# A ring of seven gather buffers instead of four, and four routing steps ahead of the first gather

## The chip, the cores and the metric

One Trainium2 chip, one of its cores. TensorE (PE) multiplies matrices, with its weight loads shown apart as PEld; VectorE (DVE), ScalarE (ACT) and GpSimd (POOL) do the elementwise work; SyncE (SP) issues most of the transfers, POOL those whose rows are picked by an index. The metric is the device time of one execution in microseconds (us), as the median of several runs.

## The reference, cut to what matters

One layer of an encoder over 512 tokens of 1024 numbers: an attention and gating half, and then PEER, a lookup of single-neuron experts. The change touches only PEER:

```
def peer(h, w_q, keys, U, V):              # h: 512 x 1024; U, V: 16384 x 1024
    ...                                    # scores against 2 x 128 keys, for 8 heads
    v1, i1 = lax.top_k(s1, 16)
    v2, i2 = lax.top_k(s2, 16)
    sc, ci = lax.top_k(cand, 16)           # cand: the 16 x 16 sums of v1 and v2
    idx = i1[ci // 16] * 128 + i2[ci % 16] # 8 heads x 16 experts a token
    gates = jax.nn.softmax(sc, axis=-1)
    u_sel = U[ids]
    a = jnp.einsum('chkd,cd->chk', u_sel, xb)
    w = jax.nn.gelu(a, approximate=False) * g
    return jnp.einsum('chk,chkd->cd', w, V[ids])
```

The layer ends with a root-mean-square norm of the sum of PEER's output (times a gate) and the residual.

## The kernel before, in words

PEER is done in two ways at once. For 352 tokens it is dense: TensorE multiplies all 16384 rows of U with the tokens (tiles a, block by block of 128 experts), a mask of gates g is multiplied in, and the products w go through all rows of V into six accumulators in PSUM (out). For the other 160 tokens the rows that the routing picked are gathered: the last 128 tokens (set "g", 128 rows each) and 32 tokens whose 128 picks are spread over four partitions each (set "x", 32 gathers). A gather brings one row of 1024 numbers to each of 128 partitions, 512 KB in all, by an indirect transfer that POOL issues; VectorE then makes a dot product of it with the token (gather_u, tile scr), or adds it, scaled, to a sum (gather_v, tile acc). There are 32 + 32 gathers for x and 128 + 128 for g.

The main loop runs over e, the 128 blocks of experts. In each e TensorE does 18 matmuls into out (v times w, in three products of high and low parts: vh, vl, wh, wl) and, for the first 98, 24 matmuls of dense_a(e + 30) (uh, ul). ScalarE makes the high parts, VectorE the low ones (u..l and w..l at L82, v..l at L1063) and the product a with g (L1066). Raw u has three buffers, raw v two, and so have the high and the low parts of u and v.

Everything for the gathered tokens stands in one list, fill, with a cost for each entry. A due time grows with each e, and entries are taken from the list, in its order, when it is their turn; they are issued after that e's v..l (issue_after). The list holds, first, the 32 gather_u of x, with one step of the routing of the g tokens behind each of the first 30 of them (16 of gb_keys, a table step, 8 of route_pick, one decode, two lookups, the gates, and gb_idx, which closes the routing's memory and opens the pool gpool2 in its place); then the gather_v of x, gather_u and gather_v of g, and the output of those tokens. VectorE runs all this in the order in which it is issued, along with its u..l, v..l and w..l: where it waits for a gathered row, they wait behind it. SyncE's queue carries u, v and g; POOL's queue in this stage carries nothing but gathers, each of which waits until VectorE has read its buffer.

Of the kernel before, what the change touches and what calls it, by code (L numbers as in the profile page):

```python
# [9 lines left out]
F32 = mybir.dt.float32  # L10
# [9 lines left out]
P = 128  # L20
D = 1024
# [12 lines left out]
XS = NS // XQ  # L34
# [27 lines left out]
def tile_kernel(ctx: ExitStack, tc: tile.TileContext, a: dict, out: bass.AP):  # L62
# [3 lines left out]
    def pool(st, name, side=None, space=None):  # L66
        kw = {} if space is None else {"space": space}
        return st.enter_context(tc.tile_pool(name=name, bufs=1, side=side, reuse_waits="tile", **kw))
# [706 lines left out]
    with ExitStack() as gs:  # L775
# [63 lines left out]
        for k in range(nu):  # L839
            e = ahead + k  # L840
            s0 = k * NG // nu
            st = {}
# [30 lines left out]
    st = {}  # L873
# [19 lines left out]
    def gb_idx():  # L893
# [2 lines left out]
        st["stack"].close()  # L896
        st["gp2"] = pool(ctx, "gpool2")

    def gather(src, ix, s, name):
        g = gp.tile([P, D], F32, name=name, tag="g", bufs=4)  # L900
        nc.gpsimd.indirect_dma_start(out=g, out_offset=None, in_=src,  # L901
                                     in_offset=bass.IndirectOffsetOnAxis(ap=ix[:, s:s + 1], axis=0))
        return g
# [14 lines left out]
    def gather_u(k, ix, gt_, n, ns):  # L918
        if n == 0:
            g_open(k, ns)  # L920
        g = gather(a["peer_u"], ix, n, f"gu{k}{n}")
        actg, wg = gs_[k]["act"], gs_[k]["w"]
        scr = gp.tile([P, D], BF16, name=f"scr{k}{n}", tag="scr", bufs=1)
        nc.vector.scalar_tensor_tensor(scr, g, 1.0, gs_[k]["h2g"], op0=ALU.mult, op1=ALU.mult,  # L924
                                       accum_out=actg[:, n:n + 1])
        if n == ns - 1:
            nc.scalar.activation(wg, actg, AF.Gelu)
            nc.vector.tensor_mul(wg, wg, gt_)

    def gather_v(k, ix, s):  # L930
        g = gather(a["peer_v"], ix, s, f"gv{k}{s}")
        if s == 0:
            gs_[k]["acc"] = (gp if k == "x" else st["gp2"]).tile([P, D], F32, name=f"acc{k}")
        accg, wg = gs_[k]["acc"], gs_[k]["w"]
        if s == 0:
            nc.vector.tensor_scalar_mul(accg, g, wg[:, 0:1])
        else:
            nc.vector.scalar_tensor_tensor(accg, g, wg[:, s:s + 1], accg, op0=ALU.mult, op1=ALU.add)  # L938
# [21 lines left out]
    def o_load(b):  # L960
        n = rows[b][1] - rows[b][0]
        if b in (1, 2):
            xr = vp.tile([P, D], F32, name=f"xr{b}", tag="vr", bufs=2)
        else:
            xr = gp.tile([P, D], F32, name=f"xr{b}", tag="g", bufs=4)
        nc.sync.dma_start(xr[:n], x2d[rows[b][0]:rows[b][1], :])
        if b in ("x", GB):
            y = gp.tile([P, D], F32, name=f"yf{b}", tag="g", bufs=4)
        else:
            y = up.tile([P, D], F32, name=f"yf{b}", tag="ur", bufs=3)  # L970
        ss = gp.tile([P, 2], F32, name=f"ssf{b}", tag="ssf", bufs=2)
        yg = st["gp2"].tile([P, 512], F32, name=f"yg{b}", tag="yg", bufs=2)
        outp[b] = (xr[:n], y[:n], ss[:n], yg[:n], n)

    def o_sum(b, hf):
# [23 lines left out]
    def output(b):  # L999
        o_load(b)  # L1000
        o_sum(b, 0)
        o_gain(b)
        o_sum(b, 1)
        o_root(b)
        o_store(b)

    route = []
# [8 lines left out]
        route.append((5.0, lambda f=f: route_lookup(st["r"], f, st["i"][f])))  # L1016
    route.append((1.2, lambda: route_gates(st["R"], st["sc"], gtg, PH)))
    route.append((0.3, gb_idx))
    fill = []
    for n in range(XS):  # L1020
        fill.append((1.3, lambda n=n: gather_u("x", idxx, gtx, n, XS)))
        if n < len(route):
            fill.append(route[n])
    fill += route[XS:]
    for n in range(XS):
        fill.append((1.3, lambda n=n: gather_v("x", idxx, n)))
    for n in range(NS):
# [13 lines left out]
    gp = pool(ctx, "gpool")  # L1041
# [44 lines left out]
    for b in range(ND):  # L1086
        o_load(b)
# [71 lines left out]
```

## Time and profile before

| | |
|---|---|
| time, median of 3 runs | 1548.93 us (1538.43, 1548.93, 1552.24) |
| the profiled execution's own time | 1542.68 us |
| its span, first to last instruction | 1540.8 us |
| PE busy | 1452.5 us, 94% of the span |
| DVE busy | 1279.7 us, 83% |
| POOL busy | 455.7 us, 30% |
| read from HBM, written | 381.24 MB, 28.28 MB: 266 GB/s over the span |

The profile is of one execution. A busy PE is not a PE at its peak, so the pace of the main loop is better read from the count of its matmuls in a stretch: one e of the first 98 is 42 of them, a later one 18. The main loop runs from 598.24 us to the end; what stands before it is the attention half, the routing of the dense tokens and the building of their gates.

### The profile page before, as it was taken

The page shows a single profiled execution, that of the slowest core. Times are in us where ns is not written, and L with a number is a line of the kernel's source. Part 1 is how long each engine was busy: PE and PEld are TensorE (multiplying, and loading weights), DVE is VectorE, ACT ScalarE, POOL GpSimd, SP SyncE. Part 2 cuts the span into 40 slices and gives each one's busy share as a digit, 9 for nine tenths or more (in the row PEclk, how much of TensorE's full clock was granted, in tenths as well). Part 3 has the DMA queues.
Part 4 walks back from the last instruction along what each step waited for, and adds up shares of the span by engine and source line. Part 5 has one row for each costly group of instructions (what it writes and reads, how often), then busy time and mean ns, then how long its engine had stood idle before and what let it go on. Part 6 is the DMA issues. An engine that isn't in the chain of part 4 may idle for free.

```text
span 1540.8 us, 21600 instructions
## 1 busy us (share of the span) xinstructions
PE 1452.5 (94%) x7623; PEld 1240.4 (81%) x7623; DVE 1279.7 (83%) x2476; ACT 638.9 (41%) x1078; POOL 455.7 (30%) x400
## 2 busy tenths in 40 slices
PE   2899999999979999999999999999999999999997
PEld 1765687887869999888888888888888888877775
DVE  6937865569899997899888888988888889888776
ACT  2543433434258895333433333333333333333333
POOL 1212100000000002222344554555545445444420
PEclk9899999999989999999999999999999999999999
DMA  9626343331235789899699999999999999998973
GB/s 368 228 93 221 122 150 137 131 98 57 97 117 148 217 241 302 309 334 326 226 358 369 367 348 360 367 361 363 357 364 361 360 361 359 374 323 298 313 266 118
DMA packets 154332, 410.94 MB, mean 267 GB/s; under 512 B 13008, under 2 KB 58720, under 8 KB 154096
## 3 DMA queue, kind: packets, MB, share of 16 engines
q1 hardware_dynamic: 100720, 216.49, 40.3%
q0 software_dynamic: 51568, 187.17, 33.7%
q10 hardware_dynamic: 1936, 5.90, 1.0%
q8 instruction: 60, 0.98, 0.3%
q14 instruction: 48, 0.39, 0.1%
HBM read 381.24 MB, written 28.28 MB: 266 GB/s over the span
## 4 chain that ended last, share of the span: by engine, by line
PE 41%; DMA 24%; DVE 16%; issue 10%; ACT 4%; POOL 4%; SPq 0%; POOLq 0%; DVEq 0%; ACTq 0%
DMA gug<-peer_u,idx 10%; DMA gvg<-peer_v,idx 8%; PE out L86 4%; PE out L87 4%; PE out L88 4%; PE pa L88 3%; PE pa L87 3%; PE pa L86 3%; POOL gvg L901 2%; DMA wada<-w_ada 2%; PE gg L822 2%; ACT o L816 2%; POOL gug L901 2%; PE q L87 1%; PE q L88 1%
## 5 line engine op out<-in xcount | busy, mean ns | idle before, releaser
L901 POOL DMA_INDIRECT gug<-peer_u,idx x128 | 169.8, 1327 | 147.5 <-DVE scrg L924 123.2
L901 POOL DMA_INDIRECT gvg<-peer_v,idx x128 | 160.2, 1251 | 170.1 <-DVE accg L938 145.7
L924 DVE SCALAR_TENSOR_TENSOR scrg<-gug,h2gg 128x1024 bf16<-128x1024 f32 x128 | 156.4, 1222 | 45.7 <-DMA gug<-peer_u,idx 44.6
L938 DVE SCALAR_TENSOR_TENSOR accg<-gvg,wgg,accg 128x1024 f32<-128x1024 f32 x127 | 163.0, 1284 | 28.8 <-DMA gvg<-peer_v,idx 27.6
L901 POOL DMA_INDIRECT gux<-peer_u,idxx x32 | 41.4, 1293 | 439.5 <-DMA u34r<-u_t 342.1
L822 PE MATMUL gg<-o,o 128*128 128x128 f32 x704 | 87.9, 279 | 2.7 <-ACT o L816 1.6
L822 PEld LDWEIGHTS gg<-o,o 128*128 128x128 f32 x704 | 85.5, 195 | 4.6 <-ACT o L816 4.6
L1066 DVE TENSOR_TENSOR a<-a,g 128x352 f32<-128x352 f32 x128 | 64.7, 516 | 3.5 <-ACT g L833 2.2
L816 ACT ACTIVATE o<-o1b,gT 128x128 f32<-128x128 bf16 x176 | 58.1, 404 | 12.9 <-PE gg L822 7.4
L155 DVE SCALAR_TENSOR_TENSOR macc<-wada,csil,macc 128x1024 f32<-128x1024 f32 x40 | 51.2, 1281 | 9.5 <-DMA wada<-w_ada 9.2
L526 ACT ACTIVATE a<-pa 128x352 f32<-128x352 f32 x128 | 58.3, 456 | 1.5 <-PE pa L88 1.4
L901 POOL DMA_INDIRECT gvx<-peer_v,idxx x32 | 41.3, 1292 | 55.8 <-DVE accx L938 32.1
L805 DVE TENSOR_TENSOR o<-iota_s,gT 128x1024 f32<-128x1024 f32 x44 | 53.5, 1216 | 0.5 <-PE gg L822 0.4
L809 DVE TENSOR_SCALAR o<-iota_s,gT 128x128 f32<-128x128 f32 x176 | 48.8, 338 | 0.0
L938 DVE SCALAR_TENSOR_TENSOR accx<-gvx,wgx,accx 128x1024 f32<-128x1024 f32 x31 | 39.8, 1284 | 8.7 <-DMA gvx<-peer_v,idxx 8.5
L831 ACT COPY st<-gg 128x512 f32<-128x512 f32 x88 | 46.2, 580 | 0.0
L924 DVE SCALAR_TENSOR_TENSOR scrx<-gux,h2gx 128x1024 bf16<-128x1024 f32 x32 | 38.7, 1210 | 4.9 <-DMA gux<-peer_u,idxx 4.9
L141 POOL DMA_DIRECT2D wada<-w_ada x32 | 17.1, 535 | 60.6 <-DVE macc L155 25.2
L165 PE MATMUL mcol<-ident_s,macc 128*128 128x128 f32 x32 | 7.2, 383 | 27.4 <-DVE macc L152 23.2
L165 PEld LDWEIGHTS mcol<-ident_s,macc 128*128 128x128 f32 x32 | 5.2, 194 | 29.1 <-DVE macc L152 18.1
L430 ACT ACTIVATE pe<-s,mx 128x512 f32<-128x512 f32 x16 | 11.0, 689 | 29.6 <-DVE mx L428 21.6
L120 POOL TENSOR_TENSOR n_r<-n_ms,nhalf 128x1 f32<-128x1 f32 (+1 forms) x5 | 3.6, 715 | 54.3 <-DVE n_ms L118 54.3
(2817 smaller groups left out, 4980.5 us busy)
## 6 DMA issues: line engine op xcount, KB each, us to landing
gd<-st SPq DMA_DIRECT2D x11, 1984.0 KB, 9.1
g<-gd SPq DMA_DIRECT2D x31, 704.0 KB, 7.6
wada<-w_ada POOLq DMA_DIRECT2D x32, 512.0 KB, 4.7
wada<-w_ada SPq DMA_DIRECT2D x16, 512.0 KB, 10.1
x<-x SPq DMA_DIRECT2D x4, 512.0 KB, 12.1
x<-x ACTq DMA_DIRECT2D x4, 512.0 KB, 5.0
x2d<-x ACTq DMA_DIRECT2D x4, 512.0 KB, 2.7
gug<-peer_u,idx POOLq DMA_INDIRECT x128, 7.4
```

Source lines behind the costliest of these rows:

```text
L86: nc.tensor.matmul(o, lhsT=lh, rhs=rh, start=first, stop=False)
L87: nc.tensor.matmul(o, lhsT=lh, rhs=rl, start=False, stop=False)
L88: nc.tensor.matmul(o, lhsT=ll, rhs=rh, start=False, stop=last)
L155: nc.vector.scalar_tensor_tensor(acc, w, csil[:, c:c + 1], acc, op0=ALU.mult, op1=ALU.add)
L526: nc.scalar.activation(t, p[:, :TD], AF.Gelu)
L805: nc.vector.tensor_tensor(o2s[n], iota.unsqueeze(1).to_broadcast([P, UT, P]), tT[:, 1, t0:t0 + UT].unsqueeze(2).to_broadcast([P, UT, P]), ...
L816: nc.scalar.activation(o1s[n][:, i, :], e[:, :, i], AF.Copy, scale=tT[:, 2, t0 + i:t0 + i + 1])
L822: nc.tensor.matmul(pgs[n][i // 4][:, i % 4 * P:(i % 4 + 1) * P], lhsT=o2[:, i, :], rhs=o1[:, i, :], start=True, stop=True)
L901: nc.gpsimd.indirect_dma_start(out=g, out_offset=None, in_=src, in_offset=bass.IndirectOffsetOnAxis(ap=ix[:, s:s + 1], axis=0))
L924: nc.vector.scalar_tensor_tensor(scr, g, 1.0, gs_[k]["h2g"], op0=ALU.mult, op1=ALU.mult, accum_out=actg[:, n:n + 1])
L938: nc.vector.scalar_tensor_tensor(accg, g, wg[:, s:s + 1], accg, op0=ALU.mult, op1=ALU.add)
L1066: nc.vector.tensor_tensor(wv3, wv3, gt[:, :, e % GE, :], op=ALU.mult)
```

## The change

Three things. The gathers take their buffers by a counter: of each seven, three (counter modulo 7 is 1, 3 or 5) go to three buffers of a new tag, g2, in gpool2, and four to the old ones, as soon as gpool2 exists; until then all go to the old four. The output's half tile yg, which had two buffers of its own in gpool2, shares the tag g2. And four routing steps stand at the head of the list, so that the routing ends four gathers earlier in it.

```diff
+    ring = [0]
+
     def gather(src, ix, s, name):
-        g = gp.tile([P, D], F32, name=name, tag="g", bufs=4)
+        ring[0] += 1
+        if "gp2" in st and ring[0] % 7 in (1, 3, 5):
+            g = st["gp2"].tile([P, D], F32, name=name, tag="g2", bufs=3)
+        else:
+            g = gp.tile([P, D], F32, name=name, tag="g", bufs=4)
...
-        yg = st["gp2"].tile([P, 512], F32, name=f"yg{b}", tag="yg", bufs=2)
+        yg = st["gp2"].tile([P, 512], F32, name=f"yg{b}", tag="g2", bufs=3)
...
-    fill = []
+    lead = 4
+    fill = route[:lead]
     for n in range(XS):
         fill.append((1.3, lambda n=n: gather_u("x", idxx, gtx, n, XS)))
-        if n < len(route):
-            fill.append(route[n])
-    fill += route[XS:]
+        if n + lead < len(route):
+            fill.append(route[n + lead])
+    fill += route[XS + lead:]
```

Three places show what this does to the order. The first is VectorE at the fourth e. MAX, MAX_INDEX and MATCH_REPLACE are routing steps, scrx4 uses the fifth gathered row gux4, and u34l is the low part that TensorE needs for dense_a(34). Before, scrx0 to scrx3 stand just ahead of these rows:

```order
L924 SCALAR_TENSOR_TENSOR scrx4_5639,actx_5467<-gux4_5637,h2gx_5462 128x1024
L542 MAX v12g_5395<-tmpg011_5631 128x8
L539 MAX v12g_5395<-sgb2_5619 128x8
L543 MAX_INDEX i12g_5396<-v12g_5395,tmpg011_5631 128x8
L540 MAX_INDEX i12g_5396<-v12g_5395,sgb2_5619 128x8
L541 MATCH_REPLACE tmpg020_5705<-v12g_5395,sgb2_5619 128x128
L924 SCALAR_TENSOR_TENSOR scrx5_5713,actx_5467<-gux5_5711,h2gx_5462 128x1024
L542 MAX v12g_5395<-tmpg020_5705 128x8
L82 TENSOR_TENSOR u34l_5718<-u34r_5715,u34h_5717 128x1024
```

And in the changed kernel, from the first gathered row to the same u34l:

```order
L931 SCALAR_TENSOR_TENSOR scrx0_5561,actx_5557<-gux0_5559,h2gx_5552 128x1024
L542 MAX v12g_5395<-tmpg021_5637 128x8
L931 SCALAR_TENSOR_TENSOR scrx1_5635,actx_5557<-gux1_5633,h2gx_5552 128x1024
L543 MAX_INDEX i12g_5396<-v12g_5395,tmpg021_5637 128x8
L82 TENSOR_TENSOR w3l_5684<-a3_2443,w3h_5683 128x352
L931 SCALAR_TENSOR_TENSOR scrx2_5707,actx_5557<-gux2_5705,h2gx_5552 128x1024
L539 MAX v12g_5395<-sgb3_5625 128x8
L931 SCALAR_TENSOR_TENSOR scrx3_5719,actx_5557<-gux3_5717,h2gx_5552 128x1024
L540 MAX_INDEX i12g_5396<-v12g_5395,sgb3_5625 128x8
L541 MATCH_REPLACE tmpg030_5711<-v12g_5395,sgb3_5625 128x128
L82 TENSOR_TENSOR u34l_5724<-u34r_5721,u34h_5723 128x1024
```

Ahead of u34l there were six gathered rows to use, now there are four, and scrx4 and scrx5 stand behind it.

The second is POOL's queue in the long run of the g gathers; DMASW0 to DMASW7 are the eight semaphores that gathers signal in turn, and each gather waits for the one of the gather that had its buffer before it. Before:

```order
L901 DMA gug88_9823<-peer_u,idx_1854 128x1024 [waits DMASW4_49,DVE_49]
L901 DMA gug89_9889<-peer_u,idx_1854 128x1024 [waits DMASW5_49,DVE_49]
L901 DMA gug90_9893<-peer_u,idx_1854 128x1024 [waits DMASW6_49,DVE_49]
L901 DMA gug91_9897<-peer_u,idx_1854 128x1024 [waits DMASW7_49,DVE_49]
L901 DMA gug92_9963<-peer_u,idx_1854 128x1024 [waits DMASW0_49,DVE_49]
```

And now:

```order
L908 DMA gug88_9823<-peer_u,idx_1854 128x1024 [waits DMASW1_49,DVE_49]
L908 DMA gug89_9889<-peer_u,idx_1854 128x1024 [waits DMASW2_49,DVE_49]
L908 DMA gug90_9893<-peer_u,idx_1854 128x1024 [waits DMASW3_49,DVE_49]
L908 DMA gug91_9897<-peer_u,idx_1854 128x1024 [waits DMASW4_49,DVE_49]
L908 DMA gug92_9963<-peer_u,idx_1854 128x1024 [waits DMASW5_49,DVE_49]
```

The semaphore that each gather waits for moved by three: gug92 waited for the gather four ahead of it and now waits for the one seven ahead.

The third is POOL's queue where gpool2 opens, at the end of the gather_u of x. Before:

```order
L901 DMA gux26_6819<-peer_u,idxx_1856 128x1024 [waits DMASW6_49,DVE_49]
L901 DMA gux27_6892<-peer_u,idxx_1856 128x1024 [waits DMASW7_49,DVE_49]
L901 DMA gux28_7029<-peer_u,idxx_1856 128x1024 [waits DMASW0_49,DVE_49]
L901 DMA gux29_7039<-peer_u,idxx_1856 128x1024 [waits DMASW1_49,DVE_49]
L901 DMA gux30_7110<-peer_u,idxx_1856 128x1024 [waits DMASW2_49,DVE_49]
L901 DMA gux31_7114<-peer_u,idxx_1856 128x1024 [waits DMASW3_49,DVE_49]
L901 DMA gvx0_7120<-peer_v,idxx_1856 128x1024 [waits DMASW4_49,DVE_49]
```

And now:

```order
L908 DMA gux26_7032<-peer_u,idxx_1856 128x1024 [waits DMASW6_49,DVE_49]
L908 DMA gux27_7036<-peer_u,idxx_1856 128x1024 [waits DMASW7_49,DVE_49]
L908 DMA gux29_7106<-peer_u,idxx_1856 128x1024 [waits DMASW0_49,DVE_49]
L908 DMA gux31_7114<-peer_u,idxx_1856 128x1024 [waits DMASW1_49,DVE_49]
L908 DMA gux28_7040<-peer_u,idxx_1856 128x1024 [waits DMAHW3_49,DMAHW5_49,DMAHW2_49,DMAHW6_49,DMAHW1_49,Activation_49]
L908 DMA gux30_7110<-peer_u,idxx_1856 128x1024 [waits PE_49]
L908 DMA gvx0_7120<-peer_v,idxx_1856 128x1024 [waits DVE_49]
```

The first rows that go to the new buffers, gux28 and gux30, wait for what used the routing's memory, and two later gathers, gux29 and gux31, moved ahead of them.

## Rows read from the trace of the kernel before

**Rows 1.** The page: what transfers moved, in 40 slices of 38.5 us.

```profile
GB/s 368 228 93 221 122 150 137 131 98 57 97 117 148 217 241 302 309 334 326 226 358 369 367 348 360 367 361 363 357 364 361 360 361 359 374 323 298 313 266 118
```

**Rows 2.** Stretches: length, busy us (instructions) by engine, clock, DMA share, GB/s.

```profile
598.24:632.88 34.64, 31.15 (x147) 27.16 (x146) 24.17 (x78) 9.19 (x12) 12.68 (x11) 0.90 0.95 337
632.88:911.73 278.85, 278.85 (x1472) 247.12 (x1472) 254.19 (x477) 104.76 (x148) 108.52 (x83) 1.00 0.91 329
911.73:1392.46 480.73, 469.17 (x2437) 408.48 (x2437) 417.06 (x527) 169.79 (x233) 246.94 (x193) 1.00 0.96 358
1392.46:1508.57 116.11, 112.59 (x475) 84.70 (x473) 91.97 (x97) 40.58 (x54) 44.60 (x33) 0.99 0.83 286
```

**Rows 3.** Who waited for whom from 590 us on: total us, times, longest.

```profile
POOL gvg L901 <- DVE accg L938: 145.7, 88, 4.9
POOL gug L901 <- DVE scrg L924: 123.2, 84, 3.8
...
DVE scrg L924 <- DMA gug<-peer_u,idx: 44.6, 43, 3.2
...
DVE accg L938 <- DMA gvg<-peer_v,idx: 27.6, 33, 2.3
```

**Rows 4.** The same view, PE alone, from 600 to 1520 us.

```profile
PE pa L88 <- DVE u34l L82: 3.5, 1, 3.5
PE out L87 <- DVE v98l L1063: 2.6, 1, 2.6
```

**Rows 5.** TensorE in order of time: start, us, operation, [idle before it].

```profile
626.48 0.66 PE L88 MATMUL pa<-h2T,u34l 128*128 128x352 f32 x1 [3.49 <-DVE u34l L82]
626.94 0.49 PE L86 MATMUL pa<-h2T,u34h 128*128 128x352 f32 x1
627.23 0.49 PE L87 MATMUL pa<-h2T,u34h 128*128 128x352 f32 x1
```

**Rows 6.** VectorE in order of time, and POOL's fifth gather.

```profile
605.07 0.49 DVE L539 MAX8 v12g<-sgb 128x8 f32<-128x128 f32 x2 [3.98 <-DMA h2gx<-h2gd]
...
607.87 1.20 DVE L1063 TENSOR_TENSOR v2l<-v2r,v2h 128x1024 fp32r<-128x1024 f32 x1
608.99 1.21 DVE L1063 TENSOR_TENSOR v3l<-v3r,v3h 128x1024 fp32r<-128x1024 f32 x1
...
621.54 1.23 DVE L924 SCALAR_TENSOR_TENSOR scrx<-gux,h2gx 128x1024 bf16<-128x1024 f32 x1 [4.87 <-DMA gux<-peer_u,idxx]
...
625.21 1.21 DVE L82 TENSOR_TENSOR u34l<-u34r,u34h 128x1024 fp32r<-128x1024 f32 x1
...
611.62 1.87 POOL L901 DMA_INDIRECT gux<-peer_u,idxx  x1 [5.06 <-DVE v12g L539]
```

**Rows 7.** The view of tile gug: from a gather's issue to its landing.

```profile
DMA to landing us min/median/max: 4.7/7.4/10.4
```

**Rows 8.** Transfers: 880 to 1360 us in slices of 12; 3 to 36 us.

```profile
GB/s 384 348 364 325 319 372 390 326 414 370 363 374 355 352 358 367 383 315 370 369 355 324 403 334 384 366 348 403 357 337 391 328 343 392 373 341 400 332 385 348
...
3.00:36.00 33.00, 6.59 (x32) 5.13 (x32) 22.86 (x26) 5.80 (x9) 5.58 (x12) 0.99 1.02 392
```

**Rows 9.** Loads of v, us to landing: after the last gather, and among gathers.

```profile
v123r<-peer_v SPq DMA_DIRECT2D x1, 512.0 KB, 3.4
...
v112r<-peer_v SPq DMA_DIRECT2D x1, 512.0 KB, 6.3
```

**Rows 10.** VectorE's v..l, TensorE's use of it, ScalarE's cast, in order of time.

```profile
759.96 1.22 DVE L1063 TENSOR_TENSOR v21l<-v21r,v21h 128x1024 fp32r<-128x1024 f32 x1
...
768.33 0.39 PE L86 MATMUL out<-v21h,w21h 128*128 128x512 f32 x1
768.56 0.39 PE L87 MATMUL out<-v21l,w21h 128*128 128x512 f32 x1
...
1117.72 0.50 PE L87 MATMUL out<-v64l,w64h 128*128 128x512 f32 x1 [0.39 <-DVE v64l L1063]
...
1418.06 1.06 ACT L1062 CAST v103h<-v103r 128x1024 fp32r<-128x1024 f32 x1
```

## The prediction

> **What bounds the kernel now.** First I read the page's slices [rows 1]: from the middle of the span the transfers move some 360 GB/s almost without a dip, and by the stretches TensorE, VectorE and the DMA engines are all busy nine tenths of the time there [rows 2]. Any of the three could hold the main loop, and a busy share does not tell which; the count of matmuls does. In the second stretch 1472 of them, 35 steps of 42, take 278.85 us: 7.967 us a step. That is the floor, TensorE never waiting. In the third stretch, steps e = 39 to 96, 58 steps take 480.73 us, 8.288 each, so 58 x (8.288 - 7.967) = 18.6 us are lost there, in crumbs. The reader should then look at who waits [rows 3, 4]: TensorE waits for low parts that VectorE makes late, VectorE waits for gathered rows (44.6 + 27.6 us for g), and POOL, which would fetch them, waits for VectorE to free a buffer (123.2 + 145.7 us). This is a circle: buffer, transfer, use, buffer.
>
> How tight is it? In the third stretch VectorE is busy 417.06 / 58 = 7.19 us a step, so at the floor it may idle 0.78 us a step; it idles 1.10. It begins with a reserve: at e = 21 v21l is done at 761.18 us and used at 768.56, 7.4 us later, while at e = 64 TensorE waits 0.39 us for v64l [rows 10]. Between those steps the reserve was eaten, and from then on each late row costs TensorE time.
>
> The circle itself: 193 gathers in 58 steps [rows 2] are 3.33 a step, one in 8.288 / 3.33 = 2.49 us, so a buffer of four goes round in 9.96 us. Of that 7.4 us are issue to landing [rows 7] and about 1.25 the use on VectorE (a gathered dot product took 1.23 us [rows 6]), 8.65 in all. The floor needs a round of 4 x 7.967 / 3.33 = 9.57 us. On average it would fit, by 0.9 us; but landings reach 10.4 us, and a row that takes 3 us longer than the median does not.
>
> **The change, part by part.** *Seven buffers.* At the floor a buffer may now go round in 7 x 7.967 / 3.33 = 16.7 us against the same 8.65: 8.1 us of slack, more than the 3.0 us by which the latest landing exceeds the median, and more than any wait of VectorE for a row (3.2 us the longest [rows 3]). Nothing else on POOL's queue is delayed: it carries only gathers there. Whether TensorE reaches its floor then hangs on the transfers: the third stretch moved 358 GB/s x 480.73 us = 172.1 MB, which in 58 x 7.967 = 462.1 us takes 372 GB/s. The page's best slice of this stretch has 374, slices of 12 us have 400, 403 and 414, and a stretch of plain loads 392 over 33 us [rows 1, 8]. So 372 can be had, if work is always queued, which is what more buffers in flight give. Ends: nothing (the rate stays at 358) and all 18.6 us. Half way, at 366 GB/s, 172.1 MB take 470.2 us and 10.5 us are won. VectorE need not lose all its idle time, only what exceeds 0.78 us a step, so I take 16, near the upper end.
>
> *The first gathers.* At e = 3 TensorE waits 3.49 us for u34l, and then its matmuls of 352 columns start 0.29 us apart for the 22 that are left of dense_a(34) [rows 5]. Elsewhere their pace is 0.16 (a step of 7.967 less 18 matmuls at 0.23 [rows 10], over 24): the granted clock, 2.4 GHz before, was at 1.2 after the idle, which makes the stretch's mean 0.90 of full speed [rows 2]. So 3.49 + 22 x 0.13 = 6.4 us. The cause is VectorE's wait of 4.87 us for the fifth gathered row, with u34l queued behind it [rows 6]; that row could not be asked for before scrx0 had freed a buffer. In the new order u34l stands behind four rows that are already there. I walk VectorE's queue in its new order from 605.07 us with the old pace [rows 6]: eleven short instructions took the 2.80 us to v2l, 0.25 each, and v2l took 1.12. So 18 routing instructions 4.5, v2l 1.12, ten more 2.5, v3l 1.12, four rows at 1.2, w3l 0.5, five routing instructions 1.25, u34l 1.13: it ends at 622.0, and TensorE wants it when the old wait began, at 622.99. The stall goes, and the low clock with it. Next late is w4l behind scrx4: gux4 is now asked for at about 615.5, when scrx0 is done, not at 611.62, and lands after the median 7.4 us at 622.9 (after 9.9, as the old one, at 625.4); VectorE comes to scrx4 at 624.3, so w4l ends between 626.7 and 627.8, and TensorE wants it at about 626.9, 24 matmuls later. So I book 5.5 of the 6.4; ends 3 and 6.4. The reserve at the following steps is about 2 us smaller, since TensorE won more than VectorE; without more idle time it holds.
>
> *The swap on POOL.* gux28, first in a new buffer, is now issued behind gux31, which waits until scrx25 is done. From there to its landing are two issues of about 1 us and 7.4 us, against some 7 us of other work on VectorE between scrx25 and scrx28 (three long instructions and about ten short ones): a wait of 2 to 3 us. It lies at about e = 20, where the reserve is 7.4 us [rows 10]: I cost it at nothing, and at 3 us if that reserve were gone. That the routing ends four gathers earlier moves no work from one step to another but within about one of them: nothing.
>
> *The end.* In the fourth stretch 26 steps of 18 matmuls at 0.23 us [rows 10] would take 107.6 us; they take 116.11 [rows 2], 8.5 more. At its start VectorE is behind (TensorE waits 2.6 us for v98l [rows 4]); with a reserve that wait goes, the small ones later hardly. I book 4, ends 0 and 6.5. The shared g2 buffers of the output hold the same number of half tiles or more: nothing. What comes after 1508.57 us is the output and stays.
>
> **Sum** against the profiled execution's own 1542.7 us: 16 + 5.5 + 4 = 25.5 us less, 1517. The ends are 3 and 31.5 less: 1540 and 1511. That execution is 6 us under the median of the runs shown; the losses are waits that vary from run to run, which more buffers should even out, so I put the new median between 1517 and 1548.9 - 25.5 = 1523: **1520 us**, and with the forecast's own range 1508 to 1532.
>
> **The rivals.** *The transfers are full already.* Then rows arrive no faster however many are asked for: the third stretch stays at 358 GB/s, and only the first stall (5.5) and 1 or 2 us at the end are won: 1536 in the profile's time, up to 1542 as a median, say 1539. For it: a DMA share of 0.96 and a rate that hardly moves from slice to slice. Against it: the 12-us slices over 400, and the low ones between them (315, 324), which look like gaps in the asking, not a cap. The Trainium skill (HBM Reference, Specifications (TRN2)) puts a core's share of its memory at about 358 GB/s, the very rate of this stretch, and says that a core streaming alone measures well above it; by the share there would be no gain there, and the rows at 392 and more speak for the second sentence.
>
> *Slower: the gathers crowd out the v loads.* A load of v lands in 3.4 us after the last gather and in 6.3 among gathers [rows 9]. In the fourth stretch its two buffers go round in landing + 1.06 (cast) + 1.22 (low part) us [rows 10], and 2 x 4.14 = 8.3 allow a landing of 6.0: it is at the edge. If up to three more gathers in flight (1.5 MB, 4 us at 392 GB/s) were served first, a step would take (6.3 + 4 + 2.3) / 2 = 6.3 us instead of 4.3, 25 x 2 = 50 us lost there against 25 won: about 1570. It decides from a landing of about 8.3 us on, where the loss reaches 25. Against it: at the pace of VectorE's queue only 33 gathers fall in 116 us, so the mean number in flight stays, rate times landing, at 33 / 116 x 7.4 = 2.1, however many buffers there are.
>
> *The lead does not do what it says.* gux4 comes late, w4l stalls TensorE at e = 4 instead, and the clock falls again: the 5.5 becomes 0, 1526.
>
> **How the numbers follow.** Chances: forecast 0.62, full transfers 0.2, the lead without effect 0.11, slower 0.07. One per cent, 15 us, is about what a measurement of this kernel can tell from no change (its three runs span 13.8 us), so faster by over 1% means under 1533.4. Faster: 0.62 x 0.95 + 0.11 x 0.7 + a little = 0.68; slower 0.07; between, 0.25. The range reaches from the forecast's lower end, 1508, to the full-transfer case, 1541.
>
> **What would show it.** In the new profile: steps e = 39 to 96 at 8.0 to 8.05 us with 370 GB/s or more; VectorE's waits for gathers from 72 us to under 30; POOL's waits for VectorE as long or longer, but harmless, since then it has seven rows ahead; no clock under 1.00 between 600 and 640 us, and u34l ahead of TensorE's need; v loads landing in under 7 us. If VectorE's waits stay near 70 us with gathers that land in 12 us or more, the transfers were full; if e = 4 has a gap, the lead failed.

## The result, and the profile after

The changed kernel takes **1520.4 us** (median of 6 runs, 1519.5 to 1524.2) against 1547.7 us of the kernel before beside it (6 runs, 1538.4 to 1552.2): ratio 0.9856, 95% interval 0.9829 to 0.9883, 1.4% faster. The forecast was 1520 in 1508 to 1541. The profiled execution spans 1518.8 us, 22.0 less than that of before.

The first view to read is again the one by stretches, cut where TensorE begins the steps e = 0, 4, 39, 97 and 123. Columns: length, busy us (instructions) of PE, PEld, DVE, ACT and POOL, granted clock, DMA share, GB/s.

```profile
599.62:629.87 30.25, 28.53 (x146) 24.31 (x145) 21.10 (x76) 9.12 (x12) 9.70 (x8) 1.00 0.92 302
629.87:912.49 282.62, 279.77 (x1473) 246.93 (x1472) 265.51 (x490) 104.69 (x148) 128.89 (x92) 1.00 0.94 349
912.49:1374.55 462.06, 462.06 (x2437) 409.52 (x2437) 424.04 (x525) 165.84 (x233) 272.18 (x194) 1.00 0.98 373
1374.55:1486.49 111.94, 110.46 (x475) 83.86 (x473) 84.30 (x89) 40.08 (x54) 35.19 (x26) 1.00 0.74 258
```

Beside [rows 2] the four lengths change by -4.39, **+3.77**, **-18.67** and -4.17 us, in all -23.5; the loop also began 1.4 us later in this execution, which no part of the change touches. In the third stretch TensorE is busy all of its 462.06 us, 58 steps of 7.967: the floor, where TensorE never waits. One number goes the wrong way, the second stretch.

The page's slices (38.0 us each), and the shares of the chain of work that ended last, engine by engine:

```profile
PEclk9999999999998999999999999999999999999999
...
GB/s 367 233 98 206 141 153 125 132 105 67 52 164 105 227 220 267 309 327 307 268 402 400 372 376 380 379 361 378 369 387 373 380 366 378 379 357 274 306 216 117
...
PE 73%; DVE 13%; DMA 6%; ACT 4%; issue 3%; POOL 0%; SPq 0%; POOLq 0%; DVEq 0%; ACTq 0%
```

The same chain before:

```profile
PE 41%; DMA 24%; DVE 16%; issue 10%; ACT 4%; POOL 4%; SPq 0%; POOLq 0%; DVEq 0%; ACTq 0%
```

Transfers held a quarter of the chain before, and 6% of it now.

At the 21st and 22nd slice, where gathers come one behind the other, the rate is 402 and 400, above anything in [rows 1]; then it settles at 373 on average, which is what the kernel needs at its floor. In slices of 12 us, from 772 to 820:

```profile
772.00:784.00 12.00, 12.00 (x67) 10.73 (x66) 11.96 (x14) 4.30 (x6) 7.17 (x6) 1.00 1.02 409
784.00:796.00 12.00, 12.00 (x64) 10.51 (x63) 11.93 (x12) 4.27 (x6) 6.97 (x6) 1.00 1.03 409
796.00:808.00 12.00, 12.00 (x67) 10.76 (x66) 10.39 (x12) 4.29 (x6) 5.36 (x5) 1.00 1.03 409
808.00:820.00 12.00, 12.00 (x63) 10.49 (x62) 11.93 (x12) 4.28 (x6) 7.15 (x6) 1.00 1.03 411
```

Four slices at the same 409 to 411, with a DMA share of 1.02 or 1.03, look like a ceiling; an experiment below asks.

The waits of the circle [rows 3], from 590 us on, and VectorE's groups on gathered rows (count, then busy us and mean ns, then idle us before them):

```profile
POOL gvg L908 <- DVE accg L945: 141.0, 83, 6.9
POOL gug L908 <- DVE scrg L931: 72.0, 36, 4.1
...
L945 DVE SCALAR_TENSOR_TENSOR accg<-gvg,wgg,accg 128x1024 f32<-128x1024 f32 x127 | 163.8, 1290 | 1.3
...
L931 DVE SCALAR_TENSOR_TENSOR scrg<-gug,h2gg 128x1024 bf16<-128x1024 f32 x128 | 156.2, 1221 | 1.3
```

VectorE idles 1.3 + 1.3 us before the gathered rows of g, against 44.6 + 27.6 us of waits for them. By the theory below that is where the 18.7 us came from. POOL still waits 213 us for VectorE, and nobody waits for POOL.

Where the second stretch loses: PE's waits from 600 to 720 us, and VectorE in order of time around e = 3 and e = 12.

```profile
PE out L87 <- DVE v12l L1071: 1.9, 1, 1.9
PE out L88 <- DVE w3l L82: 1.7, 1, 1.7
PE out L88 <- DVE w4l L82: 0.5, 1, 0.5
PE pa L88 <- DVE u44l L82: 0.4, 1, 0.4
```

```profile
615.49 0.29 DVE L539 MAX8 v12g<-sgb 128x8 f32<-128x128 f32 x1 [3.88 <-DMA sgb<-sgd]
...
617.65 1.22 DVE L1071 TENSOR_TENSOR v3l<-v3r,v3h 128x1024 fp32r<-128x1024 f32 x1
...
621.53 0.51 DVE L82 TENSOR_TENSOR w3l<-a,w3h 128x352 fp32r<-128x352 f32 x1
...
624.96 1.23 DVE L82 TENSOR_TENSOR u34l<-u34r,u34h 128x1024 fp32r<-128x1024 f32 x1
...
691.38 0.52 DVE L82 TENSOR_TENSOR w14l<-a,w14h 128x352 fp32r<-128x352 f32 x1
695.04 0.53 DVE L1074 TENSOR_TENSOR a<-a,g 128x352 f32<-128x352 f32 x1 [3.15 <-DMA g<-gd]
695.49 1.22 DVE L1071 TENSOR_TENSOR v12l<-v12r,v12h 128x1024 fp32r<-128x1024 f32 x1
```

Two waits of VectorE are new, and neither is for a gathered row. At 611.6 it stands 3.88 us for a load of scores (sgb, the third, for the fifth routing step), with v3l, w3l and u34l behind it; at 691.9 it stands 3.15 us for a block of gates g, in front of v12l. TensorE's own waits are shorter than these, because its reserve takes the rest, but the steps e = 3 and 4 exceed their floor by 2.15 + 0.80 us (before: 6.53 and 0), and e = 12 and 13 by 2.20 + 0.76 (before: 0).

In the fourth stretch ScalarE's two longest waits for a load of v are 2.6 us for v113r and 2.5 us for v116r; here v113r, which SP issued at 1431.14:

```profile
1431.14 0.33 SPq L1063 DMA_DIRECT2D v113r<-peer_v  x1
...
1439.80 1.05 ACT L1070 CAST v113h<-v113r 128x1024 fp32r<-128x1024 f32 x1 [2.61 <-DMA v113r<-peer_v]
```

That load took 8.7 us, against 6.3 in [rows 9]. The steps e = 113 and 116 lost 1.2 and 1.0 us; before, e = 105, 111 and 116 lost 0.80, 0.45 and 0.57, with waits of the same kind.

### The profile page after: what moved, and what is told of

Read it like the earlier page. It is cut to its first block, busy times and chain, and to the rows that moved or that the text cites. A ratio compares the mean times of both kernels' runs of the same rounds, so it can differ in the third digit from the quotient of the medians.

```text
span 1518.8 us, 21628 instructions
## 1 busy us (share of the span) xinstructions
PE 1439.7 (95%) x7623; PEld 1235.6 (81%) x7623; DVE 1287.3 (85%) x2476; ACT 634.6 (42%) x1078; POOL 489.4 (32%) x400
## 4 chain that ended last, share of the span: by engine, by line
PE 73%; DVE 13%; DMA 6%; ACT 4%; issue 3%; POOL 0%; SPq 0%; POOLq 0%; DVEq 0%; ACTq 0%
PE out L86 10%; PE out L88 10%; PE out L87 10%; PE pa L88 9%; PE pa L87 9%; PE pa L86 9%; DMA wada<-w_ada 2%; PE gg L822 2%; PE q L87 1%; PE q L88 1%; PE q L86 1%; ACT o L816 1%; PE yo L87 1%; PE yo L88 1%; PE yo L86 1%
## 5 line engine op out<-in xcount | busy, mean ns | idle before, releaser
L908 POOL DMA_INDIRECT gug<-peer_u,idx x128 | 200.3, 1565 | 104.6 <-DVE scrg L931 72.0
```

## The experiments

The theory: four buffers made a round (ask, land, use, ask again) that was barely short enough, and its late rows cost the third stretch; the transfers had room. Against it stand: the new order of the work, not the ring, made the gain; the number of requests in flight, not the round, decides; the transfers are full. All ratios are to the kernel before, run on the same chip.

**The two parts alone.** *seven_no_lead*:

```
-    lead = 4
+    lead = 0
```

> Seven buffers as in the change, but no routing step ahead of the first gather. If the ring alone makes the gain of the main loop, e = 39 to 96 stays at 462 us (7.97 a step); the first stall at e = 3 comes back (6.5 us over the floor instead of 3.0 at e = 3 and 4), and if the lead caused the loss at e = 12 and 13, those 3.0 us go: about 1521, within 2 us of the changed kernel, 26 under before. If the lead was worth the 5.5 us that the prediction books, and the loss at e = 12 and 13 has another cause, it takes 1524 to 1526. If a part of the gain in the main loop came from the new order that the lead gives, the third stretch takes over 466 us and the whole over 1528.

*lead_four_buf*: the lead stays, `gather` takes all rows from the four buffers of before.

```
-        if "gp2" in st and ring[0] % 7 in (1, 3, 5):
+        if False:
```

> The lead of four routing steps with four buffers as before. If the ring makes the gain: e = 39 to 96 stays at 478 to 482 us, e = 3 and 4 together lose 3 us instead of 6.5, e = 12 and 13 lose about 3: 1545 to 1549, no difference from before. If the lead is worth what the prediction books: 1542. If the new order makes a part of the gain in the main loop: the third stretch takes under 474 us and the whole under 1541.

Seven buffers without the lead: 1519.2 us, ratio 0.9833 (0.9802 to 0.9863). The lead with four buffers: 1542.6 us, 0.9996 (0.9975 to 1.0017). Their third stretches, and behind each its fourth:

```profile
914.45:1376.51 462.06, 462.06 (x2438) 409.52 (x2437) 423.89 (x525) 165.59 (x233) 272.17 (x194) 1.00 0.99 373
1376.51:1487.58 111.07, 110.26 (x475) 83.85 (x473) 84.12 (x89) 40.05 (x54) 33.92 (x26) 1.00 0.76 260
```

```profile
912.84:1392.38 479.54, 468.36 (x2437) 408.53 (x2437) 417.51 (x529) 169.75 (x233) 242.17 (x193) 1.00 0.97 360
1392.38:1509.56 117.18, 113.10 (x475) 85.81 (x473) 92.50 (x97) 40.00 (x54) 43.54 (x33) 0.97 0.84 285
```

The whole gain of the third stretch belongs to the ring, and so does that of the fourth: 97 to 122 exceed their floor by 3.2 us with seven buffers, by 9.3 with the lead alone. The lead gives at e = 3 and 4 what it takes at e = 12 and 13: without it they lose 5.3 and 0 us, with it (four buffers) 2.6 and 2.3. The lead is worth nothing that these times can show.

**How many buffers.** The rings `% 6 in (1, 4)` with two buffers of g2, `% 5 == 1` with one, and the kernel before with three:

```
-        if "gp2" in st and ring[0] % 7 in (1, 3, 5):
+        if "gp2" in st and ring[0] % 6 in (1, 4):     # six_buf
+        if "gp2" in st and ring[0] % 5 == 1:          # five_buf
```

```
-        g = gp.tile([P, D], F32, name=name, tag="g", bufs=4)
+        g = gp.tile([P, D], F32, name=name, tag="g", bufs=3)     # three_buf
```

> The changed kernel with a ring of six buffers (four and two). By the circle (a buffer may go round in 6 x 7.967 / 3.33 = 14.4 us at the floor, against 8.65 us for landing and use and 3 us more for the latest landing) six are as good as seven: third stretch 462 to 463 us, 1519 to 1522. If what counts is how many gathers are queued at any time, a third of the gain of the main loop is lost: 468 us and about 1526.

> The changed kernel with a ring of five buffers (four and one). By the circle a buffer may go round in 5 x 7.967 / 3.33 = 12.0 us against 8.65 and 3 more for the latest landing: just enough, so nearly all of the gain stays: third stretch 462 to 466 us, 1520 to 1524. If the gain grows evenly with each buffer, two thirds of it are lost: 474 us and about 1532.

> The kernel before with three row buffers. If landing takes its 7.4 us whatever is in flight, a buffer still goes round in about 8.65 us, a row comes every 2.88 us, and the 193 rows of the third stretch take 193 x 2.88 = 556 us instead of 480; with some 30 us more in the second stretch about 1640 to 1655. If the landing time is mostly the queueing of four gathers behind each other, it falls to 5.9 us or less with three, and the kernel loses little: under 1575.

Six: 1520.0 us, 0.9843 (0.9816 to 0.9871). Five: 1520.3 us, 0.9844 (0.9814 to 0.9874). Three: 1640.7 us, 1.0649 (1.0604 to 1.0694). The third stretches, in that order:

```profile
914.70:1376.77 462.07, 462.07 (x2439) 409.55 (x2437) 423.80 (x525) 165.59 (x233) 272.65 (x194) 1.00 0.99 373
```

```profile
911.51:1373.57 462.06, 462.06 (x2437) 409.52 (x2437) 422.91 (x527) 165.59 (x233) 265.83 (x194) 1.00 0.99 373
```

```profile
937.30:1481.66 544.36, 491.85 (x2438) 423.43 (x2437) 419.80 (x530) 168.60 (x233) 229.13 (x194) 0.96 0.89 317
```

Three buffers give 544.36 / 194 = 2.81 us a row, a round of 8.4 us; the prediction had worked out 8.65 from a landing of 7.4 and a use of 1.25. The totals nearly agree, but their parts do not. With three buffers, from issue to landing (tile gug, then gvg; before, both had a median of 7.4):

```profile
DMA to landing us min/median/max: 4.2/6.3/10.2
```

```profile
DMA to landing us min/median/max: 4.3/6.0/9.7
```

The landing got shorter by more than 1 us. Followed gather by gather through the third stretch, the mean round of 8.4 us is 6.4 of landing, 0.4 until VectorE comes to the row, 1.25 of use and 0.4 until POOL issues again; before, 9.9 us were 7.4, 0.8, 1.25 and 0.5. The two waits for a turn were left out of the sum. So this time speaks for the first case of the expectation, but its condition, 7.4 us whatever is in flight, does not hold.

At the floor four buffers allow a round of 4 x 2.39 = 9.6 us and five allow 12.0. Against the 8.65 of the prediction's sum that is a slack of 0.9 and 3.3 us: with the first, four buffers lose 17 to 19 us, and with the second, five lose nothing. So the average round was short enough, and more than 0.9 us of slack was needed, which fits landings that reach 3.0 us beyond their median [rows 7]. The sixth and the seventh buffer bring nothing, where a gain that grew with each buffer would have left five at about 1532.

**How far the transfers are from full.** In the kernel with five buffers 58 more loads of rows of v, which nobody reads (the rest of the computation stays):

```
+        if 38 <= e < 96:
+            dm = st["gp2"].tile([P, 256], F32, name=f"dm{e}", tag="dm", bufs=1)    # 512, 1024
+            nc.sync.dma_start(dm, a["peer_v"][e * P:(e + 1) * P, :256])
```

> Five buffers, and at each of the steps e = 38 to 95 one more load of 128 KB (rows of v once more, read by nobody). The third stretch then has 172 + 7.6 MB to move; at TensorE's floor that is 389 GB/s. If transfers can go at the 400 of the best slices, nothing is lost: third stretch 462 to 463 us. If 373 is all they give, the stretch takes 179.7 MB / 373 GB/s = 482 us. If a fuller queue only lengthens the landing of rows, so that five buffers no longer suffice, TensorE loses up to 10 us in crumbs.

> The same with 256 KB: 187.3 MB, 405 GB/s at the floor, at the edge of what the best slices show. Transfers at 400 to 410: 462 to 468 us. Transfers at most 390: 480 us.

> The same with 512 KB: 202.5 MB, 438 GB/s at the floor, which no slice of 12 us reached. The transfers are then the bound and show their own rate: at 405 to 410 the third stretch takes 494 to 500 us. If it stays at 462, they have 438 and the limit is further off.

1587.8, 1603.0 and 1606.4 us; ratios 1.031, 1.041 and 1.043. That fits no line of what was expected: 128 KB cost some 67 us over five buffers alone, and four times as much costs 86. Most of that, 48 to 66 us, went on steps before e = 39, ahead of where the loads were meant to come. The experiment had measured something else. What SP waited for between 740 and 1000 us with 128 KB, and what ScalarE waited for:

```profile
SPq L1061 <- DMA dm<-peer_v: 194.4, 57, 6.6
```

```profile
ACT v40h L1073 <- DMA v40r<-peer_v: 13.1, 1, 13.1
ACT v29h L1073 <- DMA v29r<-peer_v: 12.9, 1, 12.9
ACT v38h L1073 <- DMA v38r<-peer_v: 12.6, 1, 12.6
```

Nothing tied the loads to their steps, so SP took all 58 loads of 128 KB between 751 and 993 us, each waiting there for the landing of the one before since they share a buffer, and the loads of u and v stood behind them. So the same with 512 KB, queued right behind the load of v of its step (*load_in_step*):

```
-        nc.sync.dma_start(vraw, a["peer_v"][e * P:(e + 1) * P, :])
+        vload = nc.sync.dma_start(vraw, a["peer_v"][e * P:(e + 1) * P, :])
+        if 38 <= e < 96:
+            dm = st["gp2"].tile([P, D], F32, name=f"dm{e}", tag="dm", bufs=1)
+            with tc.issue_after(vload.ins):
+                nc.sync.dma_start(dm, a["peer_v"][e * P:(e + 1) * P, :])
```

> Five buffers and a load of 512 KB more at each of the steps e = 38 to 95, this time queued on SP right behind the load of v of the same step, so that each comes in its own step and finds its buffer long free: 202.5 MB in the third stretch, 438 GB/s at TensorE's floor, which no slice of 12 us reached. If transfers go at 400 to 410 at most, they are the bound and show their own rate: 494 to 506 us. If 373 is all they give: 543 us. If it stays at 462 to 464, 438 can be had and the transfers were nowhere near a bound.

1551.7 us, ratio 1.0079 (1.0058 to 1.0099). The third stretch is 29.3 us longer than with five buffers alone, for 30.4 MB. The stretch, the page's slices (38.8 us each), and VectorE's and SP's waits in the stretch:

```profile
913.01:1404.33 491.32, 471.21 (x2439) 408.40 (x2437) 413.61 (x520) 166.27 (x233) 225.12 (x191) 1.00 1.02 405
```

```profile
GB/s 368 226 91 223 125 142 136 130 105 49 104 109 155 220 237 265 328 335 285 312 394 371 391 409 409 410 409 409 409 408 408 397 408 409 409 382 338 311 244 119
```

```profile
DVE scrg L931 <- DMA gug<-peer_u,idx: 43.1, 65, 2.1
DVE accg L945 <- DMA gvg<-peer_v,idx: 29.3, 36, 2.0
```

```profile
SPq L1067 <- DMA dm<-peer_v: 109.0, 47, 5.0
```

Of the twelve slices from the 24th to the 35th eleven stand at 408 to 410: here is the ceiling, 409 GB/s in this mix, the rate that the changed kernel already showed from 772 to 820 us. The changed kernel needs 373, nine tenths of it. SP waited 109 us for landings of the extra loads in this run, so it is the flat rate together with a share of 1.02, not the length alone, that makes it a ceiling. Note VectorE's waits: 43.1 and 29.3 us, against 34.8 and 27.5 in this stretch of the kernel before, from the opposite cause. There the round was too long at 358 GB/s, here the transfers are full. The sums of the waits don't tell one from the other; the rate does.

**The losses that the change brought or left.** *scores_early* puts the score loads two steps and more ahead, the third and fourth of each four into the tile that later holds the sum for x:

```
+        if h % 4 > 1:
+            st["sg"][h] = st["accx"][:, h % 4 * 256:(h % 4 + 1) * 256].rearrange("p (f n) -> p f n", n=P)
+        else:
+            st["sg"][h] = st["R"].tile([P, 2, P], F32, name=f"sgb{h}", tag="sg", bufs=2)
...
-        gb_scores(0)
+        for h in range(3):
+            gb_scores(h)
...
-        if f == 0 and h + 1 < PH:
-            gb_scores(h + 1)
+        if f == 0 and 0 < h < PH - 2:
+            gb_scores(h + 2)
```

> The changed kernel with the score loads of the lead two and more steps earlier (a third and fourth place for them in the tile that later holds the sum of x rows). If VectorE's 3.9 us wait for a score load, with v3l and u34l queued behind it, is what kept the lead from its full 5.5 us, then u34l ends about 622, e = 3 and 4 together lose under 1 us instead of 3.0, and the whole takes 3 us less than the changed kernel, about 1517. If gathered rows or the next low parts are late anyway, e = 3 and 4 still lose 2 us or more and the time stays at 1520.

*gate_late* ties the multiplication by the gates to its step:

```
+        lows.append(last)
+        with tc.issue_after(lows[max(0, e - 4)].ins):
             nc.vector.tensor_tensor(wv3, wv3, gt[:, :, e % GE, :], op=ALU.mult)
```

> The changed kernel with the multiplication of the activations by the gates (line 1074) held back on VectorE until four steps before its use; the order put it up to 28 steps ahead of use, most of that between e = 5 and 13. If that early work, and the loads of g that it waits for, ate VectorE's reserve at e = 12, the loss at e = 12 and 13 (3.0 us) goes and nothing comes back, about 1517; the last 26 steps carry 24 x 0.45 = 11 us more on VectorE, which they have idle, and lose at most 2 more. If the small reserve there comes from the lead itself, the loss stays at about 3 us or moves a few steps.

*all_three* has both, and this:

```
-        if e < NE - 3:
+        if e < NE - 3 and (e < 98 or e % 5 in (0, 2)):
             vraw = vp.tile([P, D], F32, name=f"v{e}r", tag="vr", bufs=2)
         else:
             vraw = up.tile([P, D], F32, name=f"v{e}r", tag="ur", bufs=3)
```

> Both edits, and from e = 98 on the raw rows of v take turns in five buffers (the two of v and the three of u, which are free then). If the three losses are apart from each other: 3 us at e = 3 and 4, 3 us at e = 12 and 13 and 2 us at e = 113 and 116 go, about 1512, 36 under before. If they share VectorE's reserve so that one takes the place of another: 1516 to 1519.

*scores_early*: 1517.6 us, 0.9841 (0.9803 to 0.9878). e = 3 and 4 lose nothing; u34l starts 20.4 us after the loop's start (602.20) instead of 25.3:

```profile
622.64 1.21 DVE L82 TENSOR_TENSOR u34l<-u34r,u34h 128x1024 fp32r<-128x1024 f32 x1
```

Of the loss at e = 12 and 13 1.0 us is left; VectorE still waits 2.5 us for g there, so it seems that the reserve is larger. *gate_late*: 1523.0 us, 0.9864 (0.9824 to 0.9903). The loss at e = 12 and 13 is gone, as expected, but e = 97 to 122 lose 10.2 us instead of 4.0, which was not. That stretch, and ScalarE's waits for loads of v in it, the first four of 11:

```profile
1370.97:1489.11 118.14, 112.87 (x475) 83.28 (x473) 93.40 (x114) 39.90 (x54) 36.25 (x26) 1.00 0.79 277
```

```profile
ACT v114h L1071 <- DMA v114r<-peer_v: 3.9, 1, 3.9
...
ACT v110h L1071 <- DMA v110r<-peer_v: 3.8, 1, 3.8
ACT v109h L1071 <- DMA v109r<-peer_v: 3.0, 1, 3.0
...
ACT v106h L1071 <- DMA v106r<-peer_v: 2.6, 1, 2.6
```

VectorE has the multiplications to do there now (x114 instructions against x89) and, by my reading, makes v..l later, so one of the two raw buffers comes free later and the next load of v starts later: the other circle, which the rival on the v loads had described. The next run bears it out. *all_three*, with five raw buffers there, takes 1512.3 us, 0.9803 (0.9774 to 0.9832), with no wait of ScalarE for a load of v in its last stretch:

```profile
1366.97:1476.66 109.69, 109.69 (x474) 84.01 (x472) 93.02 (x113) 37.85 (x53) 33.42 (x26) 1.00 0.82 295
```

Of all steps from e = 3 to 122 only e = 122 is still more than 0.3 us over its floor, by 1.9. The span is 1509.7 us, 9.1 under the changed kernel's, and against the kernel before it is clearly faster. It and the changed kernel were timed at different times, each against the kernel before, and the two intervals overlap by a hair; what shows where the 9.1 us went is the steps: 3.0 at e = 3 and 4, 3.0 at e = 12 and 13 and 2.3 in the last 26. The loop also began 1.6 us earlier (in all these runs, whose kernels are the same ahead of it, it begins between 597.9 and 602.2 us), and what follows the last 26 steps took 0.8 longer.

## Why the prediction was right

*What bounds the kernel*: the circle, as the first part has it. The five rings show it from both sides. That three buffers give the worked-out round to 3% is in part luck: the landing was over 1 us shorter with three, and the waits for a turn on VectorE and on POOL, 0.8 us together, were left out.

*Seven buffers*: 16 us booked, 18.7 measured, the upper end of 0 to 18.6. The reason given, that VectorE need lose only the idle time beyond 0.78 us a step, holds: it still idles 462.06 - 424.04 = 38.0 us there, 0.66 a step, but none of it for gathered rows, and TensorE runs at its floor. Taking 16 and not all 18.6 was caution that nothing here called for. The condition, 372 GB/s, was met at 373. Five buffers would have done; by the prediction's own sum, which wanted 3.0 us over the 8.65, 11.65 were enough, but the text stopped at seven.

*The first gathers*: 5.5 us booked (ends 3 and 6.4), 6.53 - 2.95 = 3.6 measured between the two profiled executions; *seven_no_lead*, with the old order, lost 5.3 there, so about 1 us of this can be variation. The walk along VectorE's queue took the routing instructions at the pace of before and left out that the step that now stands ahead of v3l waits for a load of its own: the wait of 3.88 us for sgb. *scores_early* shows it, since the whole loss goes with that wait. The clock did stay at 1.00.

*"The reserve at the following steps is about 2 us smaller ... without more idle time it holds"*: this step failed. There was more idle time, 3.15 us at e = 12 for g, and the reserve did not hold: 3.0 us lost. Kernels with the lead have this loss, whether with four, five, six or seven buffers, *seven_no_lead* has not, and *gate_late* removes it. The order shows why the lead brings it: before v12l VectorE has by then multiplied the blocks up to e = 36, without the lead only up to e = 28. So nearly all that the lead won was given back nine steps later, and a term of 5.5 was in truth about 0.6. The loop won 23.5 us where 25.5 were booked: 4.9 fewer from the first gathers, 2.7 more from the ring and 0.2 more at the end. That two misses went opposite ways is luck, and so is a median within half a us of the 1520: the profiled executions differ by 22.0 us, the medians by 27.3.

*The swap on POOL*, costed at nothing, came as worked out: VectorE waits 3.1 us for gux28, where 2 to 3 were forecast, and the reserve takes it, for e = 20 keeps its floor.

```profile
759.29 1.23 DVE L931 SCALAR_TENSOR_TENSOR scrx<-gux,h2gx 128x1024 bf16<-128x1024 f32 x1 [3.12 <-DMA gux<-peer_u,idxx]
```

*The end*: 4 booked, 4.2 measured, from the ring, by the two runs with one part each.

*Full transfers*, the rival of 0.2, is refuted. The 358 GB/s of the third stretch were the rate of a circle; one core ran at 373 with seven buffers and at 409 with more to load. The Trainium skill (HBM Reference, Specifications (TRN2)) gives a core a share of about 358 GB/s and says that a core that streams alone measures well above it, about 425. These runs agree with the second in kind, with 409 measured for this mix, and that the share met the rate of before was chance, since one more buffer raised it. *Gathers crowd out the v loads*, the rival of 0.07, did not come: its price was for all 25 steps, and the stretch got shorter. Two loads (v113r at 8.7 us, v116r at 7.0) come late and cost 2.2 us, so the sign "v loads landing in under 7 us" was wrong for them; but three such steps cost 1.8 us before, and that gathers made these loads late is not shown. One more sign was wrong: POOL does not wait as long as before for VectorE but less (213 us against 269).

Left open: why landings spread as they do, and whether the landing got shorter with three buffers because fewer gathers were in flight or because the rate was lower (317 GB/s). The trace after does not resolve the landing of single gathers.

## What to carry to other kernels

Size a ring by the latest landing, not the median: round = latest landing + use, over the time between rows. Here that gives (10.4 + 1.25) / 2.39 = 4.9, so five, and each buffer beyond it only took memory; it is one kernel's evidence. Count the waits of every instruction that a reordering puts in front of a critical one, for its loads too, and follow the new order until the reserve has been rebuilt, not to the next step. When a consumer waits for rows, look first at the rate and then at the waits: rows late at 358 GB/s and rows late at 409 left much the same waits. Buffers cured the first; against the second, where the transfers are full, none were tried. A load added to an in-order queue needs a place in it, or it costs what stands behind it and not its bytes.

## What the runs showed of the hardware

A program on one core moved 409 GB/s, in eleven of twelve neighbouring slices of 39 us and with gathered rows, plain loads of 512 KB and gates mixed. A DMA share of 0.96 to 0.99 (358 to 373 GB/s) was not full; 1.02 to 1.03 was. The median time of a gather from issue to landing was 7.4 us with a ring of four at 358 GB/s, and 6.0 to 6.3 with a ring of three at 317. A gather's instruction on POOL took 229.13 / 194 = 1.18 us on average with three buffers, 1.25 to 1.28 with four and 1.40 with seven, but 1.18 again with five when the transfers were full, so it does not go by the number of buffers; no instruction of another engine waited for POOL in the third stretch, and why is open.
